# A hybrid decoder block: the low part of every third weight block is finished by an accumulating transfer

## The chip, the cores and the metric

The kernel runs on one core of a Trainium2 chip. The metric is the device time of one execution in microseconds (us). A page and a trace of one profiled execution of the kernel before are at hand, and three timed runs.

## The reference, cut to what matters

One decoder layer on 256 tokens of width 2048 in float32: a normalisation, one wide input projection, two mixers side by side (a matrix LSTM and a differential attention), their gated sum, an output projection, and then a SwiGLU feed-forward with a hidden width of 5632.

```python
def hybrid_mixer(h, w_in, ..., w_bm, w_bd, w_out, lam_init):
    proj = h @ w_in                                   # 2048 x 16400
    mq, mk, mv, mo, mi, mf, dq, dk, dv, gm, gd = split_in(proj)
    ...
    y = jax.nn.sigmoid(gm) * (hm @ w_bm) + jax.nn.sigmoid(gd) * (hd @ w_bd)
    return y @ w_out

def swiglu(h, w_gate, w_up, w_down):
    return (jax.nn.silu(h @ w_gate) * (h @ w_up)) @ w_down

def reference(x, ...):
    h = rmsnorm(x, attn_norm_w[l])
    x = x + hybrid_mixer(h, ...)
    h = rmsnorm(x, ffn_norm_w[l])
    x = x + swiglu(h, w_ffn_gate[l], w_ffn_up[l], w_ffn_down[l])
    return rmsnorm(x, final_norm_w)
```

Nearly all arithmetic is in the products of the 256 tokens with the weight matrices.

## The kernel before, in words

Every operand of a product is held as two parts in the format fp32r: a high part (the value cast to fp32r) and a low part (the value minus its high part). A product of two such operands is three matrix multiplications: high with high (line 133), high tokens with low weights (line 134), low tokens with high weights (line 135).

The kernel is one stream of 78 products on TensorE. A product makes [256 tokens x 512 columns] from 12 or 16 row blocks of weights. Two row blocks of one product are a **unit**: 12 multiplications of 128x512 on TensorE. There are 616 units. The products stand in a fixed order: `mq0 mk0 mo0 mo1 mv0 ...` (matrix LSTM), `gm`, `bm`, then `dq dk dv` (attention), `gd`, `bd`, `wo`, then `fg`, `fu` and `fd` (feed-forward).

`Feed` brings the weights. `load` fetches four row blocks (1 MB, the tile `wr_<product>`, three buffers) by a transfer on SyncE's queue. `split` makes the two parts of one unit: ScalarE casts the raw tile to the high part `wh_<product>` (line 254), VectorE subtracts that from the raw tile and writes the low part `wl_<product>` (line 255). The tiles `wh` and `wl` have five buffers each. `run` calls `split` for the unit that lies `AHEAD = 4` units ahead of the one whose multiplications are issued next, so with five buffers a cast can begin when TensorE has done the unit five before it. In the first product (`mq0`) the splits are called by hand, and so is that of the first unit of `mk0`, from a hook of `mq0`'s row block 14, just before the last sums of squares of x.

Between the multiplications stand steps of the mixers ("side" tasks: transposes, convolution, softmax, evictions). Every engine runs its instructions in the order in which the program is written.

Of the kernel before, what the change touches and what calls it, by code (L numbers as in the profile page):

```python
# [8 lines left out]
F32 = mybir.dt.float32  # L9
# [6 lines left out]
P = 128  # L16
S = 256
# [18 lines left out]
N_T2 = 9  # L36
AHEAD = 4
ORDER = (
    "mq0 mk0 mo0 mo1 mv0 mv1 mq1 mk1 mo2 mo3 mv2 mv3 gm0 gm1 gm2 gm3 bm0 bm1 bm2 bm3 "
# [7 lines left out]
def hybrid_block(ctx, tc, x, attn_norm_w, w_in, conv_w, conv_b, b_igate, b_fgate, mlstm_norm_w,  # L47
                 lambda_q1, lambda_k1, lambda_q2, lambda_k2, diff_norm_w, w_branch_m, w_branch_d,
                 w_out, ffn_norm_w, w_ffn_gate, w_ffn_up, w_ffn_down, final_norm_w, out):
    """One stream of matrix products on the tensor engine; everything else is cut into steps that are  # L50
    issued between them. Every engine's instructions run in the order in which they stand here."""
    nc = tc.nc
# [23 lines left out]

    # ---------------------------------------------------------------- steps between the products
    class Side:
        """Tasks are generators; each yields the number of further ticks to wait before its next step."""

# [33 lines left out]

    # ---------------------------------------------------------------- operands
    class Split:
        """An operand with its contraction axis on partitions: [P, 4, S] blocks, high and low parts."""

# [12 lines left out]
    def three(o, a, b, first, last):  # L131
        """o += a.T @ b by the products of their parts."""
        nc.tensor.matmul(o, lhsT=a[0], rhs=b[0], start=first, stop=False)  # L133
        nc.tensor.matmul(o, lhsT=a[0], rhs=b[1], start=False, stop=False)  # L134
        nc.tensor.matmul(o, lhsT=a[1], rhs=b[0], start=False, stop=last)  # L135

    def transpose_half(src, dst, g, pr, scale_col=None):
        """Two [S, 128] column blocks src(tt, j) into dst's row blocks, split."""
        hi, lo = dst.hi[g], dst.lo[g]
        ps = trp.tile([P, 2, S], F32, tag="tr", name="ps_tr")  # L140
        for j in range(2):
            for tt in range(TT):
                nc.tensor.transpose(ps[:, j, tt * P:(tt + 1) * P], src(tt, 2 * pr + j), ident)
        if scale_col is None:
            h = hi[:, 2 * pr:2 * pr + 2]
            nc.scalar.copy(out=h, in_=ps)
            nc.vector.tensor_tensor(out=lo[:, 2 * pr:2 * pr + 2], in0=ps, in1=h.bitcast(F32),
                                    op=ALU.subtract)
        else:
            for j in range(2):  # L150
                k = 2 * pr + j
                nc.scalar.activation(out=hi[:, k], in_=ps[:, j], func=AF.Identity, scale=scale_col(4 * g + k))
            for j in range(2):
                k = 2 * pr + j
                nc.vector.scalar_tensor_tensor(out=lo[:, k], in0=ps[:, j], scalar=scale_col(4 * g + k),
                                               in1=hi[:, k].bitcast(F32), op0=ALU.mult, op1=ALU.subtract)
# [15 lines left out]
    def turn(src, t, rate=2):  # L172
        """t [P, 4, S] = the transpose of src [P, TT, 512], by blocks of 32 x 32 on the vector engine."""
        for n in range(16):
# [27 lines left out]

    # ---------------------------------------------------------------- the products and their weights
    class Product:
        """PSUM tiles [128 tokens, 512] of xt.T @ w[rows of kts, c0:c0+512]; done(acc) takes them."""

# [6 lines left out]
    class Feed:  # L213
        """Loads of four row blocks, then splits of two, in the order of the products."""

# [26 lines left out]
        def split(self, step=2):  # L242
            p, gi, j = self.units[self.nsplit]
            i = self.part
            if i == 0:
                if p.by_token:
                    hi, lo = c4([P, 2, 512], "wht", F32R), c4([P, 2, 512], "wlt", F32R)
                else:
# [5 lines left out]
            nc.scalar.copy(out=hi[:, i:i + step], in_=r)  # L254
            nc.vector.tensor_tensor(out=lo[:, i:i + step], in0=r, in1=hi[:, i:i + step].bitcast(F32),  # L255
                                    op=ALU.subtract)
            self.part += step
# [13 lines left out]
    def run(p):  # L271
# [3 lines left out]
        for tts in ([(0,), (1,)] if p.by_token else [(0, 1)]):  # L275
            for u in p.units:
# [4 lines left out]
                for i, kt in enumerate(kts):  # L281
# [6 lines left out]
                    if p is first and kt == 0:  # L288
                        # in the order in which the parts come
                        for n, (xi, wi) in enumerate(((0, 0), (1, 0), (0, 1))):  # L290
# [10 lines left out]

    # ---------------------------------------------------------------- 1 / sqrt
    def rsqrt(v, n, name):
        """1 / sqrt(v) on [P, n], by Newton steps from an integer estimate."""
        iv = small([P, n], f"rsi{n}", I32)
# [30 lines left out]

    # ---------------------------------------------------------------- start: constants, x, first weights
    allk = list(range(NK))
# [6 lines left out]
    def load_x(c, i, n):  # L345
        """Piece i of n of column chunk c of the tokens."""
        m = 512 // n
        t = c4([P, TT, m], f"x{c}")
        nc.sync.dma_start(out=t, in_=x_v[c][:, :, i * m:(i + 1) * m])
        xs.setdefault(c, []).append(t)  # L350

    def x_cols(c, k):
        """Columns [128 k, 128 k + 128) of chunk c."""
        n = len(xs[c])
        f = k * P % (512 // n)
        return xs[c][k * n // 4][:, :, f:f + P]
# [11 lines left out]

    mask_st = cp.tile([P, S], F32, name="mask_st")   # keys on partitions, queries along the row
    mask_ts = cp.tile([P, P], F32, name="mask_ts")   # queries on partitions, keys along the row  # L370
    nc.gpsimd.memset(mask_st, 0.0)
# [17 lines left out]
    def warm_up(n):  # L389
        """Products of zeros: the tensor engine's clock rises only under load."""  # L390
        wps = accp.tile([P, 512], F32, tag="acc", name="ps_warm")
# [55 lines left out]

    # ---------------------------------------------------------------- evictions
    def tokens_of(acc, name):
# [5 lines left out]
    def values_of(acc, hi, lo):  # L455
        """The product times the token scale, as high and low parts [P, TT, 2, DV]."""
        for tt in range(TT):
# [8 lines left out]

    # ---------------------------------------------------------------- gates of the mLSTM
    gt = {}
# [11 lines left out]
    def gates_task():  # L480
# [8 lines left out]
        nc.vector.tensor_copy(out=selr, in_=sel)  # L489
        # columns per row block: [i high | f high | i low | f low], 32 apart  # L490
        wgs = [c4([P, NK // 2, P], f"wg{i}", F32R) for i in range(2)]
        for i in range(2):
# [6 lines left out]
            yield 1  # L499
        # the token scales along the row  # L500
        ps = at()
# [17 lines left out]
        for i, t in enumerate((ig, z)):  # L519
# [3 lines left out]
            nc.vector.scalar_tensor_tensor(out=t, in0=nz, scalar=bg[:, i:i + 1], in1=t, op0=ALU.add, op1=ALU.add)  # L523
        # log sigmoid(z) = min(z, 0) - log(1 + exp(-|z|))
        nc.vector.tensor_scalar(out=nz, in0=z, scalar1=-1.0, scalar2=None, op0=ALU.mult)
# [8 lines left out]
        yield  # L534
        # m_t - b_t = max(0, max over s <= t of (ig_s - b_s))
        nc.vector.tensor_tensor_scan(out=M, data0=ones, data1=A, initial=0.0, op0=ALU.mult, op1=ALU.max)
# [17 lines left out]

    # ---------------------------------------------------------------- mLSTM
    def conv_task(tok, ft0, dst):
# [148 lines left out]

    # ---------------------------------------------------------------- branch gates and the first branch
    ys, sgd = [], []
# [13 lines left out]

    # ---------------------------------------------------------------- lambda
    nlam = cp.tile([P, 1], F32, name="nlam")

    def lambda_task():
# [11 lines left out]
        yield 1  # L737
        # -(e1 - e2 + lam_init) = (e2 - lam_init) - e1
        nc.vector.scalar_tensor_tensor(out=nlam, in0=lexp[:, 1:2], scalar=-LAM_INIT, in1=lexp[:, 0:1],
                                       op0=ALU.add, op1=ALU.subtract)  # L740

    # ---------------------------------------------------------------- differential attention
    SCL = DK ** -0.5
# [94 lines left out]

    # ---------------------------------------------------------------- second branch, the sum, the residual
    yT = Split(4, "yT")  # L840
# [36 lines left out]

    # ---------------------------------------------------------------- SwiGLU, by parts of the hidden axis
    parts = [(0, 4), (4, 8), (8, 11)]
# [40 lines left out]
    def final_squares(c):  # L920
# [6 lines left out]
        if c == 2:  # L927
            for tt in range(TT):
                # the first three column blocks' part of the mean, and eps
                s = small([P, 1], f"s3_{tt}", bufs=1)  # L930
# [6 lines left out]
    def final_done(acc, tt):  # L937
# [4 lines left out]
        square_sum(t, sq)  # L942
        # an estimate from the square root, and a Newton step
        sd, v, hv, r0, h, r = (small([P, 1], f"f{i}") for i in range(6))
# [15 lines left out]

    # ---------------------------------------------------------------- the order of the products
    w = w_in[0]
# [69 lines left out]

    # ---------------------------------------------------------------- each engine in this order
    last_on = {}
# [37 lines left out]
```

## Time and profile before

| | |
|---|---|
| time, median of 3 runs | 1752.54 us (1752.36 to 1753.24) |
| span of the profiled execution | 1750.4 us |
| TensorE (PE) busy | 1739.8 us, 99% of the span |
| VectorE (DVE) busy | 1217.4 us, 70% |
| ScalarE (ACT) busy | 856.6 us, 49% |
| GpSimd (POOL) busy | 6.3 us |
| transfers | 332.08 MB, mean 190 GB/s |

The profiled execution has no time of its own beside its span; the median of the runs is 2.1 us longer than that span. Shares are averages over the whole span. A busy PE is not proof of a full one, since the ends of multiplications are modelled, so the prediction looks at the distance between their starts too.

### The profile page before, as it was taken

Reading aid. Unit: us, or ns where it says so; the run is one execution under the profiler, and the core shown is the slowest. Engines: PE = TensorE matmul, PEld = TensorE weight load, DVE = VectorE, ACT = ScalarE, POOL = GpSimd, SP = SyncE. Lnnn points to the kernel's source line nnn. Section 1 sums busy time; section 2 is a strip of 40 time slices with the busy share of each in tenths; the row PEclk is TensorE's granted clock in tenths of the full one; section 3 lists DMA queues with packets and bytes.
Section 4 is the critical chain, followed back from the end, with each engine's and each line's share of the span. In section 5 each row is a group of like instructions: output and inputs, shape, how many; then the busy total and the mean of one; then the engine's idle time right before and its main releaser. Section 6 shows DMA issues by size and latency. Waiting matters only on the chain.

```text
span 1750.4 us, 20353 instructions
## 1 busy us (share of the span) xinstructions
PE 1739.8 (99%) x7873; PEld 1443.0 (82%) x7873; DVE 1217.4 (70%) x1838; ACT 856.6 (49%) x1103; POOL 6.3 (0%) x31
## 2 busy tenths in 40 slices
PE   9999999999999999999999999999999999999998
PEld 7888888888888888888888888888888888888886
DVE  6876877875567978876597886666546666546655
ACT  7555565644345555565444554444344444344443
POOL 1000000000000000000000000000000000000000
PEclk9999999999999999999999999999999999999999
DMA  8656555655666556555666566665566665566553
GB/s 265 215 174 192 163 174 172 180 192 195 193 194 179 175 167 187 169 172 181 212 217 204 192 206 203 193 192 193 193 194 192 194 196 195 194 193 195 196 185 106
DMA packets 169872, 332.08 MB, mean 190 GB/s; under 512 B 7584, under 2 KB 9264, under 8 KB 169776
## 3 DMA queue, kind: packets, MB, share of 16 engines
q1 hardware_dynamic: 169744, 330.78, 59.8%
q8 instruction: 61, 1.00, 0.2%
q14 instruction: 35, 0.29, 0.0%
q10 hardware_dynamic: 32, 0.01, 0.0%
HBM read 328.67 MB, written 2.10 MB: 189 GB/s over the span
## 4 chain that ended last, share of the span: by engine, by line
PE 99%; DMA 0%; DVE 0%; SPq 0%; ACT 0%; issue 0%; DVEq 0%
PE acc_fd L135 5%; PE acc_fg L134 5%; PE acc_fg L133 5%; PE acc_fu L134 5%; PE acc_fu L133 5%; PE acc_fd L133 5%; PE acc_fu L135 5%; PE acc_fg L135 5%; PE acc_fd L134 5%; PE acc_mv L133 2%; PE acc_mo L133 2%; PE acc_dq L133 2%; PE acc_gm L133 2%; PE acc_gd L133 2%; PE acc_dq L135 2%; PE acc_dk L135 2%
## 5 line engine op out<-in xcount | busy, mean ns | idle before, releaser
L255 DVE TENSOR_TENSOR wl_fg<-wr_fg,wh_fg 128x1024 fp32r<-128x1024 f32 x88 | 107.8, 1225 | 85.3 <-ACT wh_fg L254 84.7
L255 DVE TENSOR_TENSOR wl_fu<-wr_fu,wh_fu 128x1024 fp32r<-128x1024 f32 x88 | 107.6, 1225 | 80.8 <-ACT wh_fu L254 80.3
L254 ACT CAST wh_fg<-wr_fg 128x1024 fp32r<-128x1024 f32 x88 | 93.0, 1057 | 142.1 <-PE acc_fu L135 66.5
L255 DVE TENSOR_TENSOR wl_fd<-wr_fd,wh_fd 128x1024 fp32r<-128x1024 f32 x82 | 100.1, 1225 | 89.7 <-ACT wh_fd L254 89.6
L254 ACT CAST wh_fd<-wr_fd 128x1024 fp32r<-128x1024 f32 x82 | 86.2, 1056 | 122.1 <-PE acc_fd L135 96.1
L254 ACT CAST wh_fu<-wr_fu 128x1024 fp32r<-128x1024 f32 x88 | 92.6, 1054 | 96.4 <-PE acc_fg L135 48.5
L133 PE MATMUL acc_fg<-wh_fg,x1Th 128*128 128x512 f32 x352 | 136.9, 389 | 0.0
L134 PE MATMUL acc_fg<-wl_fg,x1Th 128*128 128x512 f32 x352 | 136.9, 389 | 0.0
L135 PE MATMUL acc_fg<-wh_fg,x1Tl 128*128 128x512 f32 x352 | 136.9, 389 | 0.0
L133 PE MATMUL acc_fu<-wh_fu,x1Th 128*128 128x512 f32 x352 | 136.9, 389 | 0.0
L134 PE MATMUL acc_fu<-wl_fu,x1Th 128*128 128x512 f32 x352 | 136.9, 389 | 0.0
L135 PE MATMUL acc_fu<-wh_fu,x1Tl 128*128 128x512 f32 x352 | 136.9, 389 | 0.0
L133 PEld LDWEIGHTS acc_fg<-wh_fg,x1Th 128*128 128x128 f32 x352 | 66.1, 188 | 13.7
L135 PEld LDWEIGHTS acc_fg<-wh_fg,x1Tl 128*128 128x128 f32 x352 | 66.1, 188 | 13.7
L133 PEld LDWEIGHTS acc_fu<-wh_fu,x1Th 128*128 128x128 f32 x352 | 66.1, 188 | 13.7
L135 PEld LDWEIGHTS acc_fu<-wh_fu,x1Tl 128*128 128x128 f32 x352 | 66.1, 188 | 13.7
L134 PEld LDWEIGHTS acc_fu<-wl_fu,x1Th 128*128 128x128 f32 x352 | 66.1, 188 | 13.7
L134 PEld LDWEIGHTS acc_fg<-wl_fg,x1Th 128*128 128x128 f32 x352 | 66.1, 188 | 13.6
L178 DVE STREAM_TRANSPOSE turned<-g 32x256 f32<-32x256 f32 x160 | 69.7, 435 | 2.5
L255 DVE TENSOR_TENSOR wl_bm<-wr_bm,wh_bm 128x1024 fp32r<-128x1024 f32 x32 | 39.2, 1225 | 37.4 <-ACT wh_bm L254 37.3
L178 DVE STREAM_TRANSPOSE turned<-tok_dqk 32x256 f32<-32x256 f32 x128 | 55.7, 435 | 2.1
L254 ACT CAST wh_bm<-wr_bm 128x1024 fp32r<-128x1024 f32 x32 | 33.8, 1056 | 46.6 <-PE acc_bm L135 42.4
(378 smaller groups left out, 4611.4 us busy)
## 6 DMA issues: line engine op xcount, KB each, us to landing
wr_fg<-in_w_ffn_gate_dram SPq DMA_DIRECT2D x44, 1024.0 KB, 5.2
wr_fu<-in_w_ffn_up_dram SPq DMA_DIRECT2D x44, 1024.0 KB, 5.2
wr_fd<-in_w_ffn_down_dram SPq DMA_DIRECT2D x44, 1024.0 KB, 5.1
wr_mo<-in_w_in_dram SPq DMA_DIRECT2D x16, 1024.0 KB, 5.5
wr_mv<-in_w_in_dram SPq DMA_DIRECT2D x16, 1024.0 KB, 5.4
wr_gm<-in_w_in_dram SPq DMA_DIRECT2D x16, 1024.0 KB, 5.4
wr_bm<-in_w_branch_m_dram SPq DMA_DIRECT2D x16, 1024.0 KB, 5.1
wr_dq<-in_w_in_dram SPq DMA_DIRECT2D x16, 1024.0 KB, 5.4
```

What stands on the lines that cost most here:

```text
L133: nc.tensor.matmul(o, lhsT=a[0], rhs=b[0], start=first, stop=False)
L134: nc.tensor.matmul(o, lhsT=a[0], rhs=b[1], start=False, stop=False)
L135: nc.tensor.matmul(o, lhsT=a[1], rhs=b[0], start=False, stop=last)
L178: nc.vector.transpose(out=o, in_=i)
L254: nc.scalar.copy(out=hi[:, i:i + step], in_=r)
L255: nc.vector.tensor_tensor(out=lo[:, i:i + step], in0=r, in1=hi[:, i:i + step].bitcast(F32), op=ALU.subtract)
```

## The change

For the units whose number leaves 2 or 5 when divided by 6, the vector subtraction is left out. ScalarE, after the cast to the high part, writes the negated cast of the raw tile into the low part's tile; then GpSimd issues a transfer that adds the weights to it. For remainder 2 the weights come from the raw tile in SBUF, for remainder 5 they are read from DRAM once more. The first product and the last one (`by_token`) are excluded. That is 201 of 616 units: 101 from SBUF, 100 from DRAM.

```diff
+BY_DMA = {2: "sbuf", 5: "dram"}
...
             nc.scalar.copy(out=hi[:, i:i + step], in_=r)
-            nc.vector.tensor_tensor(out=lo[:, i:i + step], in0=r, in1=hi[:, i:i + step].bitcast(F32),
-                                    op=ALU.subtract)
+            by = BY_DMA.get(self.nsplit % 6) if step == 2 and not p.by_token and p is not first else None
+            if by is None:
+                nc.vector.tensor_tensor(out=lo[:, i:i + step], in0=r, in1=hi[:, i:i + step].bitcast(F32),
+                                        op=ALU.subtract)
+            else:
+
+                nc.scalar.activation(out=lo, in_=r, func=AF.Identity, scale=-1.0)
+                if by == "dram":
+                    g = self.groups[gi][1]
+                    r = p.w[:, g[j]:g[j] + 2, p.c0:p.c0 + 512]
+                nc.gpsimd.dma_start(out=lo, in_=r, accum_op=ALU.add)
```

ScalarE's instructions at the change from `mq0` to `mk0`, before: the cast of `mk0`'s first unit (`wh_mk_390`) stands between two pairs of sums of squares (`junk`).

```order
L335 ACTIVATE junk,ssx<-x_131 128x512 x2
L254 CAST wh_mk_390<-wr_mk_233 128x1024
L335 ACTIVATE junk,ssx<-x_136 128x512 x2
L254 CAST wh_mk_423<-wr_mk_233 128x1024
L452 ACTIVATE tok_cv<-acc_mq_0_144,rs_x 128x512
```

The same place after the change (lines of the changed kernel are 1 to 10 higher):

```order
L345 ACTIVATE junk,ssx<-x_131 128x512 x2
L255 CAST wh_mk_390<-wr_mk_233 128x1024
L262 ACTIVATE wl_mk_391<-wr_mk_233 128x1024
L345 ACTIVATE junk,ssx<-x_136 128x512 x2
L255 CAST wh_mk_424<-wr_mk_233 128x1024
L462 ACTIVATE tok_cv<-acc_mq_0_144,rs_x 128x512
```

One instruction came in, the negated cast `wl_mk_391`, behind the cast and ahead of the second pair of squares.

GpSimd's instructions from the end of the set-up on, before (`sel` and `gb` belong to the LSTM's gates, `vah` and `val` to its values):

```order
L1019 MEMSET one_141 128x4
L483 MEMSET sel 8x1024
L484 AFFINE_SELECT sel<-sel 8x1024
L518 MEMSET gb 8x256
L694 CAST vah<-one_141 128x2x2
```

And after:

```order
L1029 MEMSET one_141 128x4
L266 DMA wl_mk_391<-wr_mk_233 128x1024
L266 DMA wl_mk_462<-in_w_in_dram 128x2x512
L266 DMA wl_mk_508<-wr_mk_428 128x1024
L266 DMA wl_mo_571<-in_w_in_dram 128x2x512
L266 DMA wl_mo_640<-wr_mo_532 128x1024
L266 DMA wl_mo_702<-in_w_in_dram 128x2x512
L266 DMA wl_mo_761<-wr_mo_663 128x1024
L493 MEMSET sel 8x1024
```

The accumulating transfers stand in GpSimd's queue from the second product on, alternately from SBUF and from DRAM, with the few small GpSimd instructions between them.

ScalarE in the feed-forward, after the change, where `fg` passes into `fu` (before, the same casts stand without the rows of line 262):

```order
L255 CAST wh_fg_8992<-wr_fg_8888 128x1024
L255 CAST wh_fg_9015<-wr_fg_8923 128x1024
L262 ACTIVATE wl_fg_9016<-wr_fg_8923 128x1024
L255 CAST wh_fg_9036<-wr_fg_8923 128x1024
L255 CAST wh_fu_9058<-wr_fu_8958 128x1024
L255 CAST wh_fu_9078<-wr_fu_8958 128x1024
L262 ACTIVATE wl_fu_9079<-wr_fu_8958 128x1024
```

Every third cast is now followed by a negated cast of the same raw tile.

## Rows read from the trace of the kernel before

**Rows 1.** Page, parts 1 and 2: busy time, then busy tenths in 40 slices.

```profile
PE 1739.8 (99%) x7873; PEld 1443.0 (82%) x7873; DVE 1217.4 (70%) x1838; ACT 856.6 (49%) x1103; POOL 6.3 (0%) x31
...
PE   9999999999999999999999999999999999999998
...
DVE  6876877875567978876597886666546666546655
...
PEclk9999999999999999999999999999999999999999
```

**Rows 2.** Waits of TensorE: line, what it waited for, total, times, longest.

```profile
PE ps_warm L393 <- DVE ssx L387: 1.1, 1, 1.1
PE acc_mq L292 <- ACT wh_mq L254: 0.4, 1, 0.4
PE ps_x L401 <- DMA x<-in_x_dram: 0.2, 1, 0.2
```

**Rows 3.** Timeline in the feed-forward: start, duration, engine, line, operation, idle before.

```profile
1302.16 0.39 PE L134 MATMUL acc_fg<-wl_fg,x1Th 128*128 128x512 f32 x1
1302.39 0.39 PE L135 MATMUL acc_fg<-wh_fg,x1Tl 128*128 128x512 f32 x1
1302.61 0.39 PE L133 MATMUL acc_fg<-wh_fg,x1Th 128*128 128x512 f32 x1
1302.81 1.06 ACT L254 CAST wh_fu<-wr_fu 128x1024 fp32r<-128x1024 f32 x1 [1.66 <-PE acc_fg L135]
...
1303.90 1.23 DVE L255 TENSOR_TENSOR wl_fu<-wr_fu,wh_fu 128x1024 fp32r<-128x1024 f32 x1 [1.49 <-ACT wh_fu L254]
...
1313.49 0.39 PE L133 MATMUL acc_fu<-wh_fu,x1Th 128*128 128x512 f32 x1
1313.72 0.39 PE L134 MATMUL acc_fu<-wl_fu,x1Th 128*128 128x512 f32 x1
```

**Rows 4.** Timeline where mq0 passes into mk0.

```profile
27.73 1.05 ACT L254 CAST wh_mk<-wr_mk 128x1024 fp32r<-128x1024 f32 x1
...
27.98 0.39 SPq L237 DMA_DIRECT2D wr_mk<-in_w_in_dram  x1
...
28.82 1.23 DVE L255 TENSOR_TENSOR wl_mk<-wr_mk,wh_mk 128x1024 fp32r<-128x1024 f32 x1 [0.86 <-ACT wh_mk L254]
...
32.39 0.40 PE L134 MATMUL acc_mk<-wl_mk,xth 128*128 128x512 f32 x1
```

**Rows 5.** Timeline of ScalarE, then TensorE, around the shortest later window (gd).

```profile
828.44 1.99 ACT L254 CAST wh_gd<-wr_gd 128x1024 fp32r<-128x1024 f32 x2
...
836.75 0.39 PE L134 MATMUL acc_gd<-wl_gd,xth 128*128 128x512 f32 x1
```

**Rows 6.** Transfers by line: count, KB each, median us from issue to landing.

```profile
wr_fg<-in_w_ffn_gate_dram SPq DMA_DIRECT2D x44, 1024.0 KB, 5.2
...
out_dram<-x SPq DMA_DIRECT2D x8, 256.0 KB, 3.1
...
fw<-in_final_norm_w_dram SPq DMA_DIRECT2D x2, 512.0 KB, 6.3
```

**Rows 7.** Timeline of SyncE's queue around the two fw transfers.

```profile
1022.33 0.37 SPq L237 DMA_DIRECT2D wr_fu<-in_w_ffn_up_dram  x1
1022.75 0.97 SPq L905 DMA_DIRECT2D fw<-in_final_norm_w_dram  x2
```

**Rows 8.** Timeline of GpSimd: its longest instruction.

```profile
3.53 1.08 POOL L484 TENSOR_SCALAR_AFFINE_SELECT sel<-sel 8x1024 f32<-8x1024 f32 x1
```

**Rows 9.** Stretches: busy us per engine (instructions), PEclk, DMA share, GB/s.

```profile
1300.00:1316.32 16.32, 16.32 (x74) 13.52 (x73) 7.36 (x6) 7.59 (x8) 0.00 (x0) 1.00 0.62 194
...
5.00:10.00 5.00, 4.41 (x25) 3.32 (x25) 3.88 (x8) 3.58 (x9) 0.00 (x0) 1.00 1.04 360
```

**Rows 10.** Waits of SyncE's queue: what a load waited for, total, times, longest.

```profile
SPq L237 <- DVE wl_fg L255: 212.0, 42, 5.6
```

## The prediction

> **What bounds the kernel now.** I read the page's busy times and slices first. TensorE is at 99% in every slice, at the full granted clock, while VectorE stands at 70% [rows 1]. So the engine from which the change takes work is not the one that sets the end. Next I read TensorE's waits: three in the whole program, 1.7 us together, all in the first microseconds, none on a low part [rows 2]. A busy bar could still hide gaps, so I looked at the distance between the starts of multiplications in the timeline: 1302.39 to 1302.61 and 1313.49 to 1313.72 is 0.22 to 0.23 us, while VectorE works on a subtraction and while it doesn't [rows 3]. A unit of 12 multiplications takes about 2.72 us: the four units from 1302.61 to 1313.49 take 10.88 [rows 3]. TensorE is a full pipe; an earlier low part gives it nothing, a later one can only hold it up.
>
> The question is therefore how late a low part may be. In the feed-forward the cast for a unit begins at 1302.81, when TensorE has freed the buffer, and ends at 1303.87; TensorE wants that unit's low part at 1313.72 (line 134 is the first to read it) [rows 3]. Before, the subtraction is done at 1305.13, 8.6 us early. Each unit's low part thus has a window, and I followed it for each of the 201 units that change. For 182 it is as in this row or longer; 19 are shorter, those of the start and a few where ScalarE is behind with other work.
>
> **The change part by part.** VectorE loses 201 subtractions of 1.23 us [rows 3], 247 us of busy time. Worth in the sum: 0, since TensorE waits for none of them [rows 2]. The most that could come back is the 1.7 us of those waits, which lie ahead of the first changed unit.
>
> ScalarE gains 201 negated casts. None is in the trace; the nearest row is the cast of the same tile and shape, 1.06 us [rows 3]. That is 213 us more on an engine with 893 us idle [rows 1], and it comes between the cast and the transfer, so it goes off the window: 1313.72 - 1303.87 - 1.06 = **8.8 us** remain from the end of the negated cast to TensorE's need. At the start the cast of mk0's first unit ends at 28.78, the negated one would end at 29.84, and the need is at 32.39 [rows 4]: **2.55 us** remain. In gd the first of two casts from 828.44 ends about 829.5 (half of 1.99 plus the overlap), so 836.75 - 829.5 - 1.06 = **6.2 us** remain [rows 5]; it is the shortest window after the second product. Squares and the second cast behind the new ScalarE instruction at the start shift by 1.06 us; they lead to the scales of mq0's eviction, for which TensorE has two more accumulators.
>
> GpSimd gains 201 transfers. Call T the time from the end of the negated cast until TensorE may read the sum. No accumulating transfer and none issued by GpSimd stands in the trace. Its issue: SyncE's takes 0.37 us [rows 7], GpSimd's longest instruction of any kind 1.08 us [rows 8]; I take the middle, 0.7. Its travel: below, 3.1 us for half its size, a store of 256 KB [rows 6]; above, two loads of 1 MB one behind the other, 2 x 5.2 = 10.4 us [rows 6], as if it had to read source and destination and also let a load pass. The nearest row has the same size and the same company: the two fw transfers of 512 KB, issued 0.4 us behind a 1 MB load, took 6.3 us [rows 6, 7]. I take 6.3 because a load is nearly always under way in this kernel: 16.32 us hold three, of 5.2 us each [rows 6, 9]. **T = 6.3 + 0.7 = 7.0 us**, with ends of 3.5 and 11.5.
>
> With T = 7.0:
> - mk0's first unit: 7.0 - 2.55 = **4.5 us** of stall, once. Nothing can win it back, as TensorE is full from there on. The next changed units, with windows of 3.4 and 6.8 us before, get these 4.5 us on top and stay covered (7.9 and 11.3).
> - gd: 7.0 - 6.2 = **0.8 us**. The other late ones hold (from 6.96 us up).
> - All windows of 8.8 us: nothing; the cover is 1.8 us.
>
> Sum: 4.5 + 0.8 = 5.3 us on the span of 1750.4, so 1755.7. Runs lie 2.1 us above that span: **1758 us**.
>
> What the cover costs if it goes: two changed units in six are three apart and each window spans four units, so a stall at one lies inside the window of the next and feeds it, but not of the one after. Above 8.8 us the price is (T - 8.8) once in six units, about 100 times: 100 us per us. That is why the range is long above.
>
> Two other things that are late next. A raw buffer of an SBUF-fed unit is held until its transfer has read it. Loads now wait 5.0 us each for a free raw buffer (212.0 us over 42) [rows 10], and the raw tile of a group is wanted again five units, 13.6 us, after its last split: less 2.3 us for that split and 5.2 us of load there are 6 us to spare, and the transfer began one unit, 2.72 us, before that split. It can take some 9 us, so this gives way after the window, not before. And GpSimd's own instructions (gates, values) now stand between transfers; the longest, 1.08 us [rows 8], is inside the cover.
>
> **The rivals.**
> *Not slower: a short transfer.* If T is at most 6.0 us, the start costs at most 3.5 us and gd nothing: 1752.5 to 1756.0, no change that can be told (0.2% is 3.5 us here, about what a measurement tells from no change). At the low end, 3.5 us, it is 1.0 us: 1753.5. For it: 512 KB is half a load, and loads take 5.2 us. Against it: the fw rows. [...]
>
> *A standing stall.* If T is above 8.8 us, every sixth unit waits. At 9.5 us: 7.0 at the start plus 70, about 1830; at 10.0, about 1880. For it: the DRAM-fed transfer is issued when the loads of the feed stand in front of it, and the bound above is 11.5 us. From 8.8 us on this decides.
>
> [...]
>
> *The transfer engines become the bound.* In 16.32 us they are busy 0.62 of the time for three loads [rows 9], 3.4 us per MB. Two transfers of 0.5 MB add 3.4 us as copies, 0.83 in all, but 6.7 us if the destination's bytes are read as well: 16.8 us of work in 16.32. In the densest stretch 360 GB/s cost a share of 1.04 [rows 9], that is 3.0 us per MB, so the same work would need 15.2 us. It just fits; if an addition costs more than its two reads, the span grows by the excess, and 10% over is already 170 us.
>
> *Faster.* Only through the 1.7 us of the early waits or through steps that nobody waits for; I see no way to 3.5 us.
>
> **How the numbers follow.** Forecast, T from 6.0 to 7.6 us, 1756 to 1761: 0.36. Port rival, T from 7.6 to 8.8, to about 1777: 0.12. Standing stall, 1777 to 1880 and on: 0.19. Transfer engines as bound: 0.05. Short transfer, within 0.2%: 0.26. Faster by over 0.2%: 0.02. So slower 0.72, same 0.26. The range runs from 1753, the low end of T, to 1880, a T of 10; below it lie some 0.04, above it some 0.1. The likeliest case's own range is 1756 to 1761.
>
> **What would show it.** In the changed profile TensorE should have one wait of 3 to 6 us near 32 us for mk0's first low part, released by a transfer, and next to none after that; its distance of 0.23 us should stand; VectorE near 970 us busy, ScalarE near 1070; issue to landing of the accumulating transfers 6 to 7 us. I am wrong if line 134's waits repeat every sixth unit (T over 8.8), if the first transfer lands in time (T short), if the SBUF-fed and DRAM-fed transfers differ by more than 2 us, or if the loads of raw tiles become what casts wait for.

## The result and the profile after

The changed kernel takes 1844.02 us (median of three runs, 1838.77 to 1844.63) against 1752.54 us: a ratio of 1.0511, interval 1.0491 to 1.0531, so 91.5 us slower. That lies inside the range, but in the case that was given 0.19, the standing stall, and not in the likeliest one: the forecast of 1758 us is 86 us off.

The page of the changed kernel: span, busy times, transfer queues (packets, MB, share of the 16 engines) and the chain that ended last.

```profile
span 1842.9 us, 21070 instructions
...
PE 1767.3 (96%) x7873; PEld 1446.1 (78%) x7873; DVE 983.2 (53%) x1637; ACT 1044.5 (57%) x1304; POOL 218.0 (12%) x232
...
q1 hardware_dynamic: 169744, 330.78, 55.0%
q0 software_dynamic: 41744, 105.39, 30.6%
...
PE 59%; DMA 30%; issue 9%; DVE 1%; ACT 0%; SPq 0%; POOLq 0%; DVEq 0%; POOL 0%
```

Against [rows 1], VectorE lost 234 us, ScalarE gained 188 and GpSimd 212. The new fact is in the last line: 30% of the chain is now transfers. TensorE's waits say which (line 135 is the old line 134, the first to read a low part; then total us, times, longest):

```profile
PE acc_fu L135 <- DMA wl_fu<-in_w_ffn_up_dram: 13.2, 10, 1.8
PE acc_fd L135 <- DMA wl_fd<-in_w_ffn_down_dram: 8.8, 7, 2.3
...
PE acc_mk L135 <- DMA wl_mk<-wr_mk: 3.4, 1, 3.4
```

Against the three waits of [rows 2] there are now waits in nearly all products, and nearly all wait for a low part fed from DRAM. The view of waits understates them, since it counts no idle time that falls under the modelled end of the multiplication before (0.97 us in the row of 1420.76 below, where the starts give 1.13). Measured by the distance between the starts of 128x512 multiplications, as the prediction did for [rows 3], and summing what exceeds 0.227 us over the whole trace: 7.2 us before, 99.2 us after. The difference, 92.0 us, is all but 0.5 us of the change of span (1842.9 - 1750.4 = 92.5). Of the 99.2 us, 74.8 lie in 57 distances that exceed 0.227 us by more than 0.26; those are called stalls below.

The transfers by line, with the median time from issue to landing:

```profile
wr_fg<-in_w_ffn_gate_dram SPq DMA_DIRECT2D x44, 1024.0 KB, 6.8
...
wl_fg<-in_w_ffn_gate_dram POOLq DMA_DIRECT2D x16, 512.0 KB, 8.6
wl_fd<-wr_fd POOLq DMA_DIRECT2D x15, 512.0 KB, 7.3
...
wl_fu<-wr_fu POOLq DMA_DIRECT2D x14, 512.0 KB, 6.7
wl_fu<-in_w_ffn_up_dram POOLq DMA_DIRECT2D x14, 512.0 KB, 9.9
```

An SBUF-fed addition of the feed-forward takes about 7 us and fits the window of 8.8 us. A DRAM-fed one takes 8.6 to 9.9, and from the end of the negated cast 63 of the 100 take more than 8.8. The loads of `fg` went from 5.2 us [rows 6] to 6.8. One stall, followed back (timeline; start, duration):

```profile
1409.67 1.05 ACT L262 ACTIVATE wl_fu<-wr_fu 128x1024 fp32r<-128x1024 f32 x1
1410.75 0.37 SPq L238 DMA_DIRECT2D wr_fu<-in_w_ffn_up_dram  x1
1411.02 1.20 POOL L266 DMA_DIRECT2D wl_fu<-in_w_ffn_up_dram  x1 [7.27 <-ACT wl_fu L262]
...
1419.40 0.39 PE L134 MATMUL acc_fu<-wh_fu,x1Th 128*128 128x512 f32 x1
...
1420.76 0.50 PE L135 MATMUL acc_fu<-wl_fu,x1Th 128*128 128x512 f32 x1 [0.97 <-DMA wl_fu<-in_w_ffn_up_dram]
```

The negated cast ends at 1410.72 (1409.67 + 1.05). It was the last reader of that raw tile, so SyncE sends the next load into its buffer at 1410.75, and GpSimd's transfer follows at 1411.02. TensorE would have taken the low part at 1419.63 and gets it at 1420.76, 1.13 us late: T is 10.0 us. What the transfer engines did meanwhile stands in the view of transfers, cut at 1415.30:

```profile
q1 hardware_dynamic: 739, 1.48, 100.9%
...
q0 software_dynamic: 272, 0.52, 54.0%
q1 hardware_dynamic: 496, 0.98, 51.6%
```

The first line is 1411.02 to 1415.30: 739 packets of loads (queue q1) and not one of the addition (q0), all engines full. The other two are 1415.30 to 1420.80: all 272 packets of the addition. It did not share the engines with the loads issued before it; it came behind them.

### The profile page after: what moved, and what is told of

Same layout as the page of the kernel before. It is cut to its first block, busy times and chain, and to the rows that moved or that the text cites. A ratio compares the mean times of both kernels' runs of the same rounds, so it can differ in the third digit from the quotient of the medians.

```text
span 1842.9 us, 21070 instructions
## 1 busy us (share of the span) xinstructions
PE 1767.3 (96%) x7873; PEld 1446.1 (78%) x7873; DVE 983.2 (53%) x1637; ACT 1044.5 (57%) x1304; POOL 218.0 (12%) x232
## 2 busy tenths in 40 slices
DMA packets 211623, 437.52 MB, mean 237 GB/s; under 512 B 10801, under 2 KB 12481, under 8 KB 211521
## 3 DMA queue, kind: packets, MB, share of 16 engines
q0 software_dynamic: 41744, 105.39, 30.6%
## 4 chain that ended last, share of the span: by engine, by line
PE 59%; DMA 30%; issue 9%; DVE 1%; ACT 0%; SPq 0%; POOLq 0%; DVEq 0%; POOL 0%
DMA wl_fu<-in_w_ffn_up_dram 5%; DMA wl_fd<-in_w_ffn_down_dram 4%; DMA wl_fg<-in_w_ffn_gate_dram 4%; PE acc_fd L135 3%; PE acc_fg L135 3%; PE acc_fd L136 3%; PE acc_fd L134 3%; PE acc_fg L134 3%; PE acc_fg L136 3%; PE acc_fu L135 2%; DMA wl_bd<-in_w_branch_d_dram 2%; PE acc_fu L136 2%; PE acc_fu L134 2%; DMA wl_wo<-in_w_out_dram 2%; DMA wl_mo<-in_w_in_dram 2%
## 5 line engine op out<-in xcount | busy, mean ns | idle before, releaser
L258 DVE TENSOR_TENSOR wl_fu<-wr_fu,wh_fu 128x1024 fp32r<-128x1024 f32 x60 | 73.5, 1226 | 128.5 <-ACT wh_fu L255 128.3
L258 DVE TENSOR_TENSOR wl_fg<-wr_fg,wh_fg 128x1024 fp32r<-128x1024 f32 x58 | 71.1, 1225 | 124.0 <-ACT wh_fg L255 123.9
L258 DVE TENSOR_TENSOR wl_fd<-wr_fd,wh_fd 128x1024 fp32r<-128x1024 f32 x54 | 66.2, 1225 | 121.8 <-ACT wh_fd L255 121.7
L255 ACT CAST wh_bd<-wr_bd 128x1024 fp32r<-128x1024 f32 x32 | 33.7, 1052 | 44.4 <-PE acc_bd L136 39.5
```

## The experiments

The theory after this result: a DRAM-fed addition is later than its window of 8.8 us. The rivals for the cause: the bytes that all transfers move, the held raw buffers, the place of DRAM as source, and the addition itself.

**One kind alone.** The first edit keeps the SBUF-fed units, the second the DRAM-fed ones.

```diff
-BY_DMA = {2: "sbuf", 5: "dram"}
+BY_DMA = {2: "sbuf"}
```

> Only the SBUF-fed third of the change (101 transfers), the DRAM-fed units are subtracted on VectorE again. Theory (a low part that lands later than its window of 8.8 us stalls TensorE, and only the DRAM-fed ones do): the start's stall of about 3.7 us is left, little else, 1756 to 1759. Rival (the transfer engines as a whole are too busy): half of the 92 us, about 1798.

```diff
-BY_DMA = {2: "sbuf", 5: "dram"}
+BY_DMA = {5: "dram"}
```

> Only the DRAM-fed part (100 transfers). If the second read from DRAM is slow by itself: T stays near 10 us, a stall of 1 to 1.5 us at nearly all of them, 1825 to 1850. Rival (it is slow because the raw buffer that the SBUF-fed transfer holds makes two loads go out just ahead of it): T falls under 8.8 us and the time to 1753 to 1762.

Measured: SBUF-fed alone 1758.70 us, 1.0035 (1.0021 to 1.0048); DRAM-fed alone 1783.77 us, 1.0178 (1.0146 to 1.0210), between its two expected ranges and in neither. TensorE's waits with the SBUF-fed units alone:

```profile
PE acc_mk L135 <- DMA wl_mk<-wr_mk: 3.5, 1, 3.5
PE ps_warm L403 <- DVE ssx L397: 1.1, 1, 1.1
```

A row of the same kernel's transfers by line:

```profile
wl_fg<-wr_fg POOLq DMA_DIRECT2D x14, 512.0 KB, 4.8
```

With 4.8 us per addition only the predicted wait at the start is left. DRAM-fed alone there are 23 stalls, 24.7 us together. Its transfers by line:

```profile
wl_fg<-in_w_ffn_gate_dram POOLq DMA_DIRECT2D x16, 512.0 KB, 8.1
wl_fu<-in_w_ffn_up_dram POOLq DMA_DIRECT2D x14, 512.0 KB, 8.4
```

The timeline of the same kernel where one of them is issued:

```profile
1387.63 6.11 SPq L238 DMA_DIRECT2D wr_fg<-in_w_ffn_gate_dram  x2
1387.90 1.19 POOL L266 DMA_DIRECT2D wl_fu<-in_w_ffn_up_dram  x1 [15.12 <-ACT wl_fu L262]
```

The kinds differ by more than 3 us, and alone they cost 6.3 + 31.3 = 38 us, not 91: the rest arises between them. A load goes out 0.27 us ahead of the addition here too.

**Which: the source or the place?** Units that leave 5 are the second of two in a raw tile, so their negated cast frees the buffer; units that leave 2 are the first. The next edit moves the DRAM-fed additions to the first units; the one after doubles them there, as many as the change has; the third has DRAM at both places.

```diff
+BY_DMA = {2: "dram"}
```

> A DRAM-fed half alone, but at the units of remainder 2 (the first unit of a raw tile), where the raw tile comes free 2.7 us after the transfer has gone out and not just before it. If a load that goes out just ahead makes the DRAM-fed transfers slow (8.1 to 8.4 us at remainder 5): 5 to 6.5 us to landing and 1757 to 1761. If reading from DRAM itself is slow: about 8 us and 1770 to 1790.

```diff
+BY_DMA = {0: "dram", 2: "dram"}
```

> A third of the units again (remainders 0 and 2), all DRAM-fed, but all at the first unit of a raw tile, so that no load goes out just ahead of any of them and none holds a raw buffer. If the place against the loads decides: 6 to 7.5 us to landing and 1758 to 1768. If the bytes on the transfer engines decide: about 1799, as with all DRAM-fed at remainders 2 and 5.

```diff
+BY_DMA = {2: "dram", 5: "dram"}
```

> All 201 transfers read from DRAM, so that none holds a raw buffer, and as many bytes move as in the change. If the load on the transfer engines makes the DRAM-fed ones later with the other half than alone (8.6 to 9.9 us against 8.1 to 8.4): 1835 to 1870. If it is the raw buffers that the SBUF-fed ones hold, and the loads queued behind that: 1780 to 1815, twice the 31 us of the DRAM-fed half at most.

Measured: 1759.14 us, 1.0037 (1.0022 to 1.0051); 1773.55 us, 1.0115 (1.0039 to 1.0191); 1799.26 us, 1.0265 (1.0246 to 1.0283). The first kernel's transfers:

```profile
wl_fd<-in_w_ffn_down_dram POOLq DMA_DIRECT2D x15, 512.0 KB, 6.1
...
wl_fu<-in_w_ffn_up_dram POOLq DMA_DIRECT2D x14, 512.0 KB, 5.8
```

The same source and size as in the DRAM-fed half, 101 transfers against 100, and 2.3 us less: the place makes the difference. From DRAM instead of from SBUF costs 1.0 to 1.3 us (5.8 to 6.1 against 4.8 to 4.9 in the SBUF-fed half). The packets show how. First the DRAM-fed half, of the transfer issued at 1387.90 (1387.90 to 1391.90, then 1392.40 to 1396.50):

```profile
q1 hardware_dynamic: 410, 0.84, 76.5%
...
q0 software_dynamic: 271, 0.52, 70.8%
q1 hardware_dynamic: 280, 0.55, 36.5%
```

For 4 us after the issue only the load's packets move. In the kernel with the addition at the first unit, the transfer of 1391.11 has its first packets by 1393.40 (1392.90 to 1393.40):

```profile
q1 hardware_dynamic: 86, 0.16, 82.8%
q0 software_dynamic: 9, 0.02, 35.4%
```

Over all transfers of each kernel, the median time from issue to the first packets (3% of them) is 4.8 us at the second unit, behind a load issued 0.27 us earlier, and 2.1 us at the first unit, 2.64 us behind its load. The loads' packets are pieces of 2 KB, 512 to a load, and the rows above show the addition behind them. Why its own packets start later, no run here tells.

The doubled kernel answers for the sheer bytes. It moves as many as the change, 437.52 MB, and loses 20 us, not 91. In the stretch from 1300 to 1500 us of the feed-forward it loses nothing (columns as in [rows 9]; first the kernel before, then the doubled one):

```profile
1300.00:1500.00 200.00, 200.00 (x884) 165.68 (x883) 128.01 (x156) 87.17 (x90) 0.00 (x0) 1.00 0.61 195
...
1300.00:1500.00 200.00, 200.00 (x884) 165.68 (x883) 99.92 (x133) 110.21 (x115) 28.63 (x24) 1.00 0.93 256
```

The same stretch of the changed kernel:

```profile
1300.00:1500.00 200.00, 190.91 (x833) 155.35 (x832) 85.04 (x104) 100.58 (x103) 23.85 (x24) 1.00 0.86 243
```

884 multiplications as before, against 833, at a higher share of the transfer engines, 0.93 against 0.86. The expectation of 1758 to 1768 us was missed by 6: 11 stalls, 12.6 us, are left over the whole kernel, 3.9 us of it at the start, one of 2.7 us in `mv` and one of 2.5 in `fg`. The one in `mv` has a load 1.0 us ahead of its addition instead of 2.6; the one in `fg` has its loads at the usual distances, and why it comes stays open.

**Held raw buffers.** Now all additions read the raw tile, so that each holds its buffer.

```diff
+BY_DMA = {2: "sbuf", 5: "sbuf"}
```

> All 201 transfers read the raw tile in SBUF. If the DRAM source is the cause: T of 7 us for all, about 1758. If held raw buffers and queued loads are the cause: loads go out later still, casts wait for them, 1800 to 1900. If the mere load of the transfer engines is the cause: about 1840 as with the change.

Measured: 1863.05 us, 1.0630 (1.0600 to 1.0661). ScalarE's largest sum of waits for loads:

```profile
ACT wh_fd L255 <- DMA wr_fd<-in_w_ffn_down_dram: 94.5, 23, 8.8
```

The waits of SyncE's queue in the same kernel:

```profile
SPq L238 <- DMA wl_fd<-wr_fd: 231.0, 28, 10.2
```

The casts now wait for loads, and the loads for additions (up to 10.2 us in `fd`): slower than the change, with the faster source. In the changed kernel the same hold works through the order. There SyncE's waits include 140.1 us for SBUF-fed additions in `fd` alone (15 times, up to 10.6 us); the load so held back goes out shortly before the next one, and the DRAM-fed addition comes behind two. Two loads were issued within 4 us ahead of it in 78 of its 100 cases, in 4 of 100 in the DRAM-fed half; packets of loads between issue and first own packets: 775 and 505 (medians). With DRAM at both places no addition reads a raw buffer, and the loss is half the change's, 47 us against 91, with all the bytes.

**The addition.** The transfer copies instead of adding, in both kinds.

```diff
-                nc.gpsimd.dma_start(out=lo, in_=r, accum_op=ALU.add)
+                nc.gpsimd.dma_start(out=lo, in_=r)
```

> The 201 transfers copy the weights over the negated part and add nothing (so the low part is wrong): the same source bytes, no read of the destination. If the addition's second read is what fills the transfer engines: their share falls from 0.86 to about 0.75, the DRAM-fed transfers land in under 8.5 us and the time is 1756 to 1775. If the addition costs nothing: about 1844 as with the change.

Measured: 1757.59 us, 1.0029 (1.0018 to 1.0040). The transfer queue of GpSimd and two rows of its transfers:

```profile
q0 software_dynamic: 41744, 105.39, 17.6%
...
wl_fg<-in_w_ffn_gate_dram POOLq DMA_DIRECT2D x16, 512.0 KB, 6.2
wl_fd<-wr_fd POOLq DMA_DIRECT2D x15, 512.0 KB, 3.7
```

The packets and bytes of the change, and 17.6% of the engines in place of 30.6%: with the addition the time of a packet nearly doubles (median from 99 to 178 ns for 2 KB, from 174 to 328 ns for 4 KB). The copies land 2.4 to 3.7 us sooner, raw buffers come free sooner, the loads of the feed-forward are back at 5.1 us, and two stalls are left, 2.7 us at the start and 0.9 in `bd`. The DRAM-fed copy still comes behind a load, with its first packets 4.1 us after issue; so the place alone doesn't make the stall; the place and the addition's own time do together.

**The window.** If lateness against 8.8 us is all, a wider window must give time back at unchanged bytes. First the negated cast is put ahead of the high cast, 1.05 us more; then the low part is made when the unit before is split, with a sixth buffer for low parts.

```diff
-            nc.scalar.copy(out=hi[:, i:i + step], in_=r)
...
+            if by is None:
+                nc.scalar.copy(out=hi[:, i:i + step], in_=r)
...
                 nc.gpsimd.dma_start(out=lo, in_=r, accum_op=ALU.add)
+                nc.scalar.copy(out=hi[:, i:i + step], in_=self.raw[gi][:, j + i:j + i + step])
```

> In the changed units ScalarE writes the negated part first and the high part after it, so each transfer starts 1.05 us earlier and the window grows from 8.8 to 9.9 us. Theory (each stall is T less the window): some 55 stalls of 1.3 us mean shrink by up to 1.05 us each, to 1785 to 1805. Rival (the transfer engines' total load sets the pace): under 10 us better, 1835 to 1844.

```diff
+        def low_early(self, n):
+            p, gi, j = self.units[n]
+            lo = wp.tile([P, 2, 512], F32R, tag="wl", name=f"wl_{p.name}", bufs=6)
+            r = self.raw[gi][:, j:j + 2]
+            nc.scalar.activation(out=lo, in_=r, func=AF.Identity, scale=-1.0)
...
+                if self.by_dma(self.nsplit) is not None:
+                    self.low_early(self.nsplit)
```

> All 201 transfers of the change, but each is prepared and issued one unit earlier (six buffers for the low part, one buffer less in the pool of the side tasks): the window grows from 8.8 to about 11.5 to 12.5 us. Theory (latency against the window): 1753 to 1762. Rival (the transfer engines are the bound): 1820 or more, since the same bytes move.

Measured: 1805.91 us, 1.0307 (1.0286 to 1.0328), 38 us off the change's loss for 1.05 us of window; and 1766.23 us, 1.0076 (1.0061 to 1.0091), 78 us off for some 3.7 us of window (a unit of 2.72 and a cast). The first is 1 us above its expected range, the second 4. In the second kernel 87 of the 201 additions still take more than 8.8 us from the end of the negated cast, but only 8 stalls are left.

Both edits also move the loads around the additions, and that shows more of the place. In the second kernel 75 of the 100 DRAM-fed additions have no load in the 4 us ahead of them, and yet they are of two kinds. One of each (timeline):

```profile
1338.35 1.20 POOL L257 DMA_DIRECT2D wl_fg<-in_w_ffn_gate_dram  x1 [7.29 <-ACT wl_fg L253]
1338.67 0.37 SPq L238 DMA_DIRECT2D wr_fg<-in_w_ffn_gate_dram  x1
...
1354.67 1.20 POOL L257 DMA_DIRECT2D wl_fu<-in_w_ffn_up_dram  x1 [7.26 <-ACT wl_fu L253]
1355.97 0.37 SPq L238 DMA_DIRECT2D wr_fu<-in_w_ffn_up_dram  x1
```

The same two in the view of transfers (1338 to 1339.9 and 1354 to 1356.4), with the time to landing:

```profile
wl_fg<-in_w_ffn_gate_dram POOLq DMA_DIRECT2D x1, 512.0 KB, 9.6
...
wl_fu<-in_w_ffn_up_dram POOLq DMA_DIRECT2D x1, 512.0 KB, 5.7
```

In the first the load goes out 0.32 us behind the addition, in the second 1.30 us. With a load up to 0.78 us behind (30 of the 75) the first packet of the addition moves 3.1 to 5.2 us after its issue, and it lands after 8.4 to 11.2 us. With the next load 0.87 us behind or later (45) the first packet moves after 1.9 us (once 3.5), and the addition lands after 5.7 to 8.4. So the load did not have to be issued first: the packets of these additions started no sooner than 1.9 us after their issue, and a load that followed within 0.78 us still went in front. The first edit fits this: there the high cast frees the raw tile, the load goes out 0.67 us behind the addition (median) and not 0.27 ahead, and DRAM-fed additions land after 9.7 us against 9.0 in the change (medians of 100), so that part of the wider window is lost again.

The second kernel's transfer engines are fuller in the stretch of before (0.89 against 0.86):

```profile
1300.00:1500.00 200.00, 198.91 (x878) 164.31 (x877) 99.13 (x131) 109.30 (x115) 25.89 (x25) 1.00 0.89 256
```

So it is the lateness that costs, not the transfers' length as such and not the bytes. The gain of VectorE's relief doesn't show even where the lateness is nearly gone.

**The rest of the sum.** Without the transfer, all other parts of the change stay; then the SBUF-fed kernel without changed units in the second product; then 2 KB pieces for the SBUF-fed transfer, the piece size of the DRAM-fed one.

```diff
-                nc.gpsimd.dma_start(out=lo, in_=r, accum_op=ALU.add)
```

> The subtraction is gone and the negated cast is there, but no transfer follows (the low part is wrong). Theory (VectorE's relief is worth nothing and ScalarE's extra work costs nothing): 1752.5 within 2 us. Rival (the relief gives something back): under 1749. Rival (ScalarE's 201 instructions delay TensorE): over 1756.

```diff
+BY_DMA = {2: "sbuf"}
...
-            by = BY_DMA.get(self.nsplit % 6) if step == 2 and not p.by_token and p is not first else None
+            by = BY_DMA.get(self.nsplit % 6) if step == 2 and not p.by_token and p is not first and p is not prods[1] else None
```

> The SBUF-fed half alone, and not in the second product (mk0) either, whose first unit has a window of 2.55 us. Theory (the 6 us of the SBUF-fed half are the start's stall of 3.7 us and the half clock that follows it): 1752 to 1754. Rival (a general cost of the transfers that every unit pays): 1757 to 1759.

```diff
+BY_DMA = {2: "sbuf"}
...
-                nc.gpsimd.dma_start(out=lo, in_=r, accum_op=ALU.add)
+                nc.gpsimd.dma_start(out=lo, in_=self.raw[gi][:, 0:4:2], accum_op=ALU.add)
```

> The SBUF-fed half alone, but the transfer takes rows 0 and 2 of the raw tile instead of two neighbouring ones (wrong rows), so its pieces are 2 KB as with the DRAM-fed ones, not 4 KB. The SBUF-fed half landed in 4.9 us, the DRAM-fed half in 8.1 to 8.4. If the number of pieces makes the difference: 7 to 8.5 us to landing, 1765 to 1785. If the source does: about 5 us, 1758 to 1760.

Measured: 1752.44 us, 1.0002 (0.9992 to 1.0011); 1754.07 us, 1.0008 (0.9999 to 1.0017); 1759.12 us, 1.0037 (1.0021 to 1.0052). The first shows that 201 subtractions less on VectorE are worth nothing and 201 casts more on ScalarE cost nothing. The second shows that most of the loss of the SBUF-fed kernel, 4.6 of 6.3 us, sat in the second product. In the third the additions land after 5.0 to 5.3 us instead of 4.8 to 4.9, so pieces of 2 KB account for a few tenths of the source's 1.0 to 1.3 us, and the time is the same. None of the kernels that compute the whole layer beats the kernel before; the best of them, 1754.07 us, can't be told from it.

## Why the prediction was right, and where it was not

**VectorE's relief, 0 us:** right; the kernel without the transfer shows it. So is ScalarE's cost of nothing but 1.06 us of each window.

**The start, 4.5 us:** the place and kind were right, the size near. The timeline of the changed kernel:

```profile
29.85 1.06 ACT L262 ACTIVATE wl_mk<-wr_mk 128x1024 fp32r<-128x1024 f32 x1
31.22 0.99 POOL L266 DMA_DIRECT2D wl_mk<-wr_mk  x1 [28.64 <-ACT wl_mk L262]
33.23 0.50 PE L134 MATMUL acc_mk<-wh_mk,xth 128*128 128x512 f32 x1
...
37.17 0.50 PE L135 MATMUL acc_mk<-wl_mk,xth 128*128 128x512 f32 x1 [3.44 <-DMA wl_mk<-wr_mk]
```

From the end of the negated cast (30.91) to the low part (37.17) T is 6.3 us, and the stall is 37.17 - 33.46 = 3.7 us. In the SBUF-fed half, where this stall and one of 0.3 us are all that is left, the whole cost is 6.3 us; 1.7 us of it is the clock (below).

**gd, 0.8 us:** did not come. That addition is SBUF-fed and was short there, 4.7 us from issue to landing: it landed at 866.43, and TensorE read it at 869.75 without a wait.

**T = 7.0 us for both kinds:** this is the step that failed. For SBUF-fed additions it held: 0.3 us from cast to issue, and 6.7 to 7.3 us from issue to landing, 7.0 to 7.6 together (5.1 without the other kind). For DRAM-fed ones it is 0.3 + 8.6 to 9.9 = 8.9 to 10.2 us, past the window of 8.8. The prediction took the fw row, 6.3 us, a plain transfer issued 0.4 us behind a load, and kept the second read, of the destination, and two loads "one behind the other" for the upper bound; that was nearer in time, though no run shows the second read by itself. The row was right for a copy: the DRAM-fed copy, 0.27 us behind its load, landed after 6.1 to 6.2 us. What it put at nothing in the 7.0 is the addition: in the same place, alone of its kind, it lands after 8.1 to 8.4 us, 2 us more, and with the SBUF-fed ones beside it after 8.6 to 9.9. The DRAM-fed addition has that company as a rule, since at every second unit of a raw tile the negated cast itself frees the buffer and the load goes out at that moment.

**The price above 8.8 us, 100 us per us:** about right. T exceeds 8.8 us in 63 of the 100 DRAM-fed additions, by 75 us in all, and the 51 stalls that end with one of them are 66 us; the loss is 91.5. For 1.05 us more of window 38 us came back, while the median T of the DRAM-fed additions rose from 9.3 us to 10.0. The standing stall, 1777 to 1880, is thus what came true, by the mechanism named for it (the loads stand in front).

**The raw buffer that "gives way after the window, not before":** right for the casts, which in the changed kernel wait for loads no more than before (8.8 us in 4 waits, 10.4 in 5 before), but not the whole of it. Its hold delays loads all through the program and bunches them ahead of the DRAM-fed additions, and with all additions on raw tiles it is the worst kernel of all.

**The transfer engines as bound:** not reached. The work for an addition was put between 15.2 and 16.8 us of 16.32, a share of 0.93 to 1.03; it is 0.93 in the doubled kernel, which loses nothing in that stretch.

**The other rivals.** The port rival, T from 7.6 to 8.8 us: no run shows what it adds to T, a GpSimd that is late to issue; in the two timelines of the changed kernel its issue begins 0.30 to 0.31 us after the negated cast ends (1409.67 + 1.05 to 1411.02, 29.85 + 1.06 to 31.22), and of all 201 only 7 begin 0.74 to 1.19 us after it. What the runs show in its place is time after the issue, 8.6 to 9.9 us to the landing of the DRAM-fed additions. A short transfer: true of the copy from SBUF, 3.7 us; the addition in the same place takes 7.3 (4.8 without the DRAM-fed ones).

Of the four signs named for being wrong, two appeared: waits of the first reader of low parts all through the program, and kinds that differ by 2 to 3 us. The first transfer did not land in time, and in the changed kernel casts did not come to wait for loads; they did with all additions on raw tiles, and the negated casts that were made a unit earlier did. One reading was loose: the last of the 40 slices shows TensorE under 90%, and the others only 90% or more; nothing hangs on it.

What stays open: how much of the DRAM-fed additions' further 0.5 to 1.5 us, from the DRAM-fed half to the change, is due to the second load ahead and how much to the SBUF-fed addition's own use of the engines. In the changed kernel the 19 with one load in the 4 us ahead land after 8.5 us (median) and the 78 with two after 9.1, against 8.3 in the DRAM-fed half; no run has the one without the other.

## What to carry to other kernels

The step that moved here from a computing engine to a transfer traded a steady time, 1.22 to 1.23 us for the 88 subtractions of `wl_fu` in the kernel before, for one that depends on what is issued around it, 5.1 to 10.4 us from issue to landing for the 28 additions of `wl_fu` in the changed kernel. Look in the trace for who frees a buffer at that same moment: here that load went in front, even when it was issued up to 0.78 us later. With TensorE a full pipe, 201 subtractions less on VectorE were worth nothing (1752.44 us against 1752.17 for the kernel before, measured beside it), and the only question was the latest arrival against the window, for each kind of transfer by itself. If the transfer is wanted all the same, put it where no load is due (1759.14 us against 1783.77 for the DRAM-fed halves) and start it a unit earlier (1766.23 against 1844.02) before touching its bytes.

## What had not been expected of the hardware

Some stalls cost more than their length. In the changed kernel, around a stall in `fu` (timeline):

```profile
1099.25 0.39 PE L134 MATMUL acc_fu<-wh_fu,x1Th 128*128 128x512 f32 x1
1102.29 0.50 PE L135 MATMUL acc_fu<-wl_fu,x1Th 128*128 128x512 f32 x1 [2.66 <-DMA wl_fu<-wr_fu]
...
1102.98 0.63 PE L134 MATMUL acc_fu<-wh_fu,x1Th 128*128 128x512 f32 x1
1103.40 0.63 PE L135 MATMUL acc_fu<-wl_fu,x1Th 128*128 128x512 f32 x1
```

And the stretches after it (time, then TensorE's busy us and multiplications; the granted clock is the third number from the end):

```profile
1102.98:1106.40 3.42, 3.42 (x10) 2.70 (x9) 0.00 (x0) 0.00 (x0) 0.00 (x0) 0.54 1.05 317
1106.40:1108.60 2.20, 2.20 (x12) 1.77 (x11) 0.75 (x1) 1.05 (x1) 0.00 (x0) 1.00 1.05 402
```

After 2.8 us without a multiplication the granted clock fell from 1.00 of full speed to 0.54 in the first of these stretches, 0.50 from 1102.72 to 1106.12: the multiplications stand 0.43 us apart instead of 0.23, and the ten from 1102.29 to 1106.28 take 3.99 us where 2.27 would do, 1.7 us more. This happened five times in the changed kernel (0.50 for 3.4 us each, from 37.8, 396.2, 1020.8, 1102.7 and 1266.6), about 8.5 us of its loss, each time behind a stall of 2.1 to 3.7 us, but not behind every such stall: 2.4 us in `bd` at 946.8 and 2.2 us in `fd` at 1576.1 left the clock at 1.00. It happened once in the SBUF-fed half, behind the stall at the start, and makes 1.7 of the 2.6 us that this kernel lost beyond that stall of 3.7 us.

An addition on the way held GpSimd longer than a copy: its issue takes 0.88 us from SBUF and 1.20 us from DRAM against 0.55 and 0.71 us. The difference between the two goes by the pieces and not by the source, since the SBUF-fed addition in pieces of 2 KB takes about as long (1.18 us in its kernel's timeline at 1391.02).
